# First squares of x earlier, weights of the value products 96 bytes further in longer rows, smaller first loads, and the last bank added in three parts

## The chip, the cores and the metric

The kernel runs on one core of one Trainium2 chip. The metric is the device time of one launch in microseconds (us), as the median of several runs. The engines are named as in the profile: PE (TensorE, with PEld for its weight loads), DVE (VectorE), ACT (ScalarE), POOL (GpSimd) and SP (SyncE, which here only starts DMAs).

## What is computed

One layer (DEPTH is 1) of a decoder trunk on 256 tokens of width 2048, in float32:

```python
h = rms_norm(x, g_mix)
qa, ka, va, qb, kb, vb, qc, kc, vc = split(h @ w_in)        # 2048 -> 6144
x = x + concat(diff_attention(qa, ka, va), moba_attention(qb, kb, vb), dilated_attention(qc, kc, vc)) @ w_out
x = x + memory_cross_attention(rms_norm(x, g_cross), rms_norm(mem, g_mem), w_cq, w_ckv, w_co)
x = x + conv_glu_ffn(rms_norm(x, g_ffn), w_up, conv_w, conv_b, w_down)   # d_ff 5632
out = rms_norm(x, g_final)
```

## The kernel before

**Tiling.** Every weight matrix is read once, in pieces of 1 MB (a tile `raw`, 128 partitions x 2048 floats, four buffers). A piece is worked off in two halves of 128 x 1024. Since PE multiplies at its fast rate only in the shortened type fp32r, each half is split into a high part (`hi`, made on ACT by `split_hi`) and the rest (`lo` = raw - hi, made on DVE by `split_lo`); each has five buffers of 128 x 1024. The activations are split in the same way (`hT`: 256 columns high, 256 columns low for each of 16 blocks of the contraction). A product then is high x high + low x high + high x low.

**Three forms of product.** `wstat_chunk` (q, k, w_out, w_up, ...) holds the weights still and streams `hT`: for each weight block one matmul over 512 columns (L295) and one over 256 (L302); where the 512 are not wanted together, L297, L298 and L302 do 256 each. `astat_chunk` (the values: three chunks of 512 columns and two of 256 from w_in, two of 256 from w_ckv) holds `hT` still and streams `hi`, `lo` and `hi` (L341 to L343). `down_mm` (w_down) holds the FFN's activations `ah`, `al` and streams `hi`, `lo`, `hi` (L851 to L853). In `astat_chunk` the streamed operand begins at the start of a `hi` or `lo` tile; in the layout of the program that start lies 64 bytes past a multiple of 128, for all ten tiles, and the held slices of `hT` lie 96 past one. In `wstat_chunk` it is the other way round (96 streamed, 64 held); in `down_mm` 64 streamed, 0 held.

**Order.** Every engine works its queue strictly in the order of the program, which the kernel writes by hand: a loop over the half pieces i runs `split_hi` for the half that is four ahead, the functions registered with `before(i)`, `split_lo`, the matmuls of half i, and those registered with `after(i)`. Chunk 0 is the first chunk of w_in (halves 0 to 7); its four results stand in four PSUM banks of the ring `acc` (five banks), and chunk 1 takes the fifth bank and then the four of chunk 0 again, each as soon as `merge` has read it: ACT copies one half of a bank to `mg` (L354), DVE adds the other (L355).

**The factor of x's norm** comes from `square_part` (ACT squares four blocks of x into `sq`, L223; for c = 1, 2, 3 DVE adds it to the first, L227) and `norm_factors` (DVE folds the sum twice, L236; PE sums over the partitions with two matmuls against `ones`, L241; DVE, POOL and PE make `rcol` and `rrow`). The parts stand behind halves 5, 6, 7 and 8, the fold before half 10.

**Start.** x comes in six loads by two or four blocks (`load_x`), mixed with the first pieces (`load_block` for two quarters of piece 0, `load_half` for halves, `load` for whole pieces from piece 3, which SP starts last of these). `put_x` makes the high and low part of two blocks of `hT`.

**End.** The last two pieces of w_down are worked off bank by bank (t is the half of the tokens, n the quarter of the columns): DVE adds the bank to x (L900), ACT squares the sum (`square_sum`, L265), DVE multiplies by the gain (`gained`, L873). For (t, n) = (1, 3) the last two pieces come in two halves of 256 columns: the first into the bank itself, the add then goes over all 512 columns; the second into a bank of its own, added over 256 (L902). Then POOL makes the factor (L915) and `finish` scales and stores: for t = 1 the quarters 0 and 1 on ACT (L862), 2 and 3 on DVE (L864), four stores of 256 KB (L869) on SP.

Of the kernel before, what the change touches and what calls it, by code (L numbers as in the profile page):

```python
# [11 lines left out]
F32 = mybir.dt.float32  # L12
# [50 lines left out]
def trunk(ctx, tc, x, mem, w_in, w_out, diff_lambda, rel_bias_table, w_cq, w_ckv, w_co, w_up, conv, w_down,  # L63
# [36 lines left out]
    class Piece:  # L100
        def __init__(self, srcs, mm, extra=None):
            self.srcs, self.mm, self.extra = srcs, mm, extra
            self.raw = None
            self.parts = [None, None]
# [33 lines left out]

    def split_hi(p, h):
        hi = wpool.tile([P, HALF], F32R, tag="hi", name="hi", bufs=NSPLIT)  # L140
        lo = wpool.tile([P, HALF], F32R, tag="lo", name="lo", bufs=NSPLIT)
# [137 lines left out]
    def wstat_chunk(w, col0, src, evac, korder=tuple(range(KD)), bank=acc_tile, wide=True):  # L279
# [5 lines left out]
        def mm(pi):  # L285
            def f(p, h):
# [18 lines left out]
                if cur[0] <= 2:  # L305
                    for f in (high, low):
                        for j in range(2):
                            for n in range(4):
                                f(n, j)
                    return  # L310
# [11 lines left out]
    def astat_chunk(w, col0, ncol, src, evac, korder):  # L322
# [25 lines left out]
        for pi in range(last + 1):  # L348
            pieces.append(Piece(sources(w, korder[pi * nk:(pi + 1) * nk], col0, ncol), mm(pi)))
# [496 lines left out]
    def down_mm(p, k, h, t, n, c0=0, c1=512, own=None):  # L846
# [6 lines left out]
        PE.matmul(o, al, wh, start=False, stop=(k == KF - 1))  # L853
# [4 lines left out]
    def finish(n, t, og, r):  # L858
        col = slice(n * 512, (n + 1) * 512)
        if t:  # L860
            if n < 2:
                ACT.activation(og[:, col], og[:, col], AF.Copy, scale=r)  # L862
            else:
                DVE.scalar_tensor_tensor(og[:, col], xtok(t, n), r, gfin["t"][:, col], op0=ALU.mult, op1=ALU.mult)  # L864
# [10 lines left out]
    def down(k):  # L875
        def f(p, h):
# [9 lines left out]
            elif k == KF - 1 and h == 1:  # L886
                done = None
                for t in range(NT):
# [5 lines left out]
                    for i, (n, c0, c1) in enumerate(parts_of):  # L894
                        own = any_tile()[:, :c1 - c0] if c0 else None
# [3 lines left out]
                        if own is None:  # L899
                            DVE.tensor_tensor(xtok(t, n), outs[t, n], xtok(t, n), op=ALU.add)  # L900
                        else:
                            DVE.tensor_tensor(xc, own, xc, op=ALU.add)  # L902
# [4 lines left out]
                        if not t or n < 2:  # L907
# [9 lines left out]
                for n in (2, 0, 3, 1):  # L917
                    finish(n, *done)
# [26 lines left out]
    load_x(0, 2)  # L945
    load_block(ACT, pieces[0], 0)
    load_block(SP, pieces[0], 1)
    ACT.copy(small(1, "first", 1), mhalf)
    load_x(2, 2)
    load_half(pieces[0], 1)  # L950
# [25 lines left out]
    put_x(0)  # L976
    p = pieces[0]
    p.parts[0] = hi, lo = [wpool.tile([P, HALF], F32R, tag=t, name=t, bufs=NSPLIT) for t in ("hi", "lo")]
# [102 lines left out]
```

## Time and profile before

| | |
|---|---|
| median of 3 runs | 1244.48 us (1242.91 to 1245.76) |
| the profiled execution | 1244.53 us, of it 1242.7 us span |
| PE busy | 1229.7 us, 99% of the span |
| DVE, ACT, POOL busy | 67%, 51%, 1% |
| mean granted clock of PE | 0.996 |
| HBM | 230 MB read, 2.1 MB written |

Times in rows count from the span's start; what lies outside the span is 1.8 us. A matmul's row shows its start and its modelled length; matmuls overlap, so their pace is read from one start to the next.

### The profile page before, as it was taken

The numbers are of one execution on the slowest core, as the hardware profiler recorded it, in microseconds if no ns is written. First come the engines' busy times: TensorE is split into PE (matmuls) and PEld (weight loads), VectorE is DVE, ScalarE is ACT, GpSimd is POOL, SyncE is SP. The second block draws the span as 40 slices with busy tenths as digits, with TensorE's granted clock in tenths as the row PEclk, the third lists the DMA queues.
The fourth block names the chain that finished last, engine by engine and source line by source line (L and its number), as shares of the span: only waits on it lengthen the run. The fifth ranks groups of instructions, "written<-read, shape, count | busy, mean of one in ns | idle before, by whom it ended". The sixth has DMA issues, their size and how long they took to land.

```text
span 1242.7 us, 17626 instructions
## 1 busy us (share of the span) xinstructions
PE 1229.7 (99%) x6934; PEld 1072.0 (86%) x6934; DVE 830.9 (67%) x1351; ACT 630.3 (51%) x981; POOL 14.2 (1%) x23
## 2 busy tenths in 40 slices
PE   8999999999999999999999999999999999999997
PEld 7888888988888899888888888888888888888885
DVE  7755667567568877776767768767677755554555
ACT  7445656556455656545444445444444544444444
POOL 0000000000000000000000000000000000000001
PEclk9999999999999999999999999999999999999998
DMA  9665554555566555565565565565656555555541
GB/s 345 209 195 190 175 178 163 184 168 173 177 216 218 170 169 166 202 206 173 169 203 183 190 198 178 182 203 190 197 176 203 185 188 204 180 192 203 180 160 68
DMA packets 104835, 233.26 MB, mean 188 GB/s; under 512 B 4208, under 2 KB 14768, under 8 KB 98992
## 3 DMA queue, kind: packets, MB, share of 16 engines
q1 hardware_dynamic: 104576, 231.85, 55.7%
q8 instruction: 54, 0.88, 0.3%
q10 hardware_dynamic: 144, 0.26, 0.1%
q14 instruction: 29, 0.24, 0.1%
q0 software_dynamic: 32, 0.02, 0.0%
HBM read 230.00 MB, written 2.12 MB: 187 GB/s over the span
## 4 chain that ended last, share of the span: by engine, by line
issue 58%; PE 37%; DVE 2%; DMA 1%; ACT 0%; POOL 0%; SPq 0%; POOLq 0%; DVEq 0%; ACTq 0%
PE acc L295 16%; PE acc L302 8%; PE acc L341 3%; PE acc L343 3%; PE acc L342 3%; DMA raw<-in_w_in 1%; PE at L401 1%; DVE lo L149 1%; PE at L420 0%; DMA xin<-in_x 0%; PE at L444 0%; PE acc L298 0%; PE acc L297 0%; DVE hT L197 0%; PE at L472 0%
## 5 line engine op out<-in xcount | busy, mean ns | idle before, releaser
L149 DVE TENSOR_TENSOR lo<-raw,hi 128x1024 fp32r<-128x1024 f32 x423 | 517.2, 1224 | 352.5 <-ACT hi L142 352.0
L142 ACT CAST hi<-raw 128x1024 fp32r<-128x1024 f32 x423 | 443.1, 1049 | 465.6 <-PE acc L295 273.3
L295 PE MATMUL acc<-hT,hi 128*128 128x512 f32 x1776 | 624.8, 394 | 2.5 <-DVE mg L355 1.9
L302 PE MATMUL acc<-hT,lo 128*128 128x256 f32 x1840 | 511.7, 280 | 0.0
L295 PEld LDWEIGHTS acc<-hT,hi 128*128 128x128 f32 x1776 | 334.0, 188 | 77.1 <-DVE mg L355 2.2
L302 PEld LDWEIGHTS acc<-hT,lo 128*128 128x128 f32 x1840 | 345.2, 188 | 0.3
L295 PE MATMUL at<-hT,hi 128*128 128x512 f32 x528 | 187.5, 392 | 0.0
L302 PE MATMUL at<-hT,lo 128*128 128x256 f32 x528 | 147.6, 280 | 0.0
L295 PEld LDWEIGHTS at<-hT,hi 128*128 128x128 f32 x528 | 99.2, 188 | 21.8
L302 PEld LDWEIGHTS at<-hT,lo 128*128 128x128 f32 x528 | 99.1, 188 | 0.0
L851 PE MATMUL acc<-hi,ah 128*128 128x512 f32 (+1 forms) x222 | 87.0, 392 | 0.0
L853 PE MATMUL acc<-hi,al 128*128 128x512 f32 (+1 forms) x222 | 86.6, 390 | 0.0
L852 PE MATMUL acc<-lo,ah 128*128 128x512 f32 (+1 forms) x222 | 85.7, 386 | 0.0
L341 PE MATMUL acc<-hi,hT 128*128 128x256 f32 (+1 forms) x224 | 75.0, 335 | 0.0
L343 PE MATMUL acc<-hi,hT 128*128 128x256 f32 (+1 forms) x224 | 73.9, 330 | 0.0
L342 PE MATMUL acc<-lo,hT 128*128 128x256 f32 (+1 forms) x224 | 73.8, 330 | 0.0
L788 ACT ACTIVATE y<-y 128x256 f32<-128x256 f32 x44 | 18.5, 419 | 66.4 <-DVE y L784 66.3
L851 PE MATMUL at<-hi,ah 128*128 128x512 f32 x132 | 52.0, 394 | 0.0
L853 PE MATMUL at<-hi,al 128*128 128x512 f32 x132 | 51.7, 392 | 0.0
L852 PE MATMUL at<-lo,ah 128*128 128x512 f32 x132 | 51.2, 388 | 0.0
L853 PEld LDWEIGHTS acc<-hi,al 128*128 128x128 f32 x222 | 41.7, 188 | 9.6
L852 PEld LDWEIGHTS acc<-lo,ah 128*128 128x128 f32 x222 | 41.7, 188 | 9.2
(159 smaller groups left out, 1005.0 us busy)
## 6 DMA issues: line engine op xcount, KB each, us to landing
raw<-in_w_up SPq DMA_DIRECT2D x88, 1024.0 KB, 5.1
raw<-in_w_in SPq DMA_DIRECT2D x45, 1024.0 KB, 5.2
raw<-in_w_down SPq DMA_DIRECT2D x44, 1024.0 KB, 4.9
raw<-in_w_out SPq DMA_DIRECT2D x12, 1024.0 KB, 5.2
raw<-in_w_ckv SPq DMA_DIRECT2D x8, 1024.0 KB, 5.3
raw<-in_w_out SPq DMA_DIRECT2D x8, 512.0 KB, 4.8
raw<-in_w_cq SPq DMA_DIRECT2D x4, 1024.0 KB, 5.3
raw<-in_w_co SPq DMA_DIRECT2D x4, 1024.0 KB, 5.3
```

The lines of the kernel that those rows point to most:

```text
L142: ACT.copy(hi, p.raw[:, h * HALF:(h + 1) * HALF])
L149: DVE.tensor_tensor(lo, p.raw[:, h * HALF:(h + 1) * HALF], hi.bitcast(F32), op=ALU.subtract)
L295: PE.matmul(accs[n], w, x, start=(i == 0), stop=False)
L302: PE.matmul(accs[n][:, :S], lo[:, j, n * P:(n + 1) * P], src()[:, korder[i], :S], start=False, stop=(i == len(korder) - 1))
L341: PE.matmul(o, xh, hi[:, j, :], start=(i == 0), stop=False)
L342: PE.matmul(o, xh, lo[:, j, :], start=False, stop=False)
L343: PE.matmul(o, xl, hi[:, j, :], start=False, stop=(i == len(korder) - 1))
L401: PE.matmul(out, a[u], b[w], start=first and i == 0, stop=last and i == 2)
L788: after(cur[0] + 1 + n, lambda: ACT.activation(gate[k], gate[k], AF.Silu))
L851: PE.matmul(o, ah, wh, start=(k == first), stop=False)
L852: PE.matmul(o, ah, wl, start=False, stop=False)
L853: PE.matmul(o, al, wh, start=False, stop=(k == KF - 1))
```

## The change

- Both kinds of split tile get rows of 1056 floats instead of 1024 (`part_tiles`), of which a piece uses 1024 from `shift` on; the pieces of `astat_chunk` get a shift of 24 floats, all others 0. The memory for it comes out of a scratch area that is made 8 KB smaller. In the new layout the ten tiles start 64 bytes past a multiple of 128 as before, the shifted operands 32 past one; the held slices of `hT` stay at 96 and of `ah`, `al` at 0. Each tile now starts 128 bytes further against `hT` than the tile before it; before, all had the same place within 4096 bytes.
- x's squares stand behind halves 1, 1, 3 and 4, so the adds before 2, 4 and 5, and the fold before 7, its matmuls behind 7.
- The first two blocks of x come in two loads and the second half of piece 0 in two; the preparation of piece 0 goes block by block, and half 0's matmuls too.
- Ahead of the last banks DVE adds bank (1, 3), which holds all but the last two pieces, to x; both of its halves then go to banks of their own and are added over 256 columns. For t = 1 only quarter 0 is multiplied by the gain ahead and finished on ACT; quarters 1 to 3 go to DVE. The quarters 2 and 0 are finished and stored in halves, six stores in all.

```diff
-        def __init__(self, srcs, mm, extra=None):
-            self.srcs, self.mm, self.extra = srcs, mm, extra
+        def __init__(self, srcs, mm, extra=None, shift=0):
+            self.srcs, self.mm, self.extra, self.shift = srcs, mm, extra, shift
...
+    def part_tiles(p):
+
+        return [wpool.tile([P, HALF + 32], F32R, tag=t, name=t, bufs=NSPLIT)[:, p.shift:p.shift + HALF] for t in ("hi", "lo")]
+
     def split_hi(p, h):
-        hi = wpool.tile([P, HALF], F32R, tag="hi", name="hi", bufs=NSPLIT)
-        lo = wpool.tile([P, HALF], F32R, tag="lo", name="lo", bufs=NSPLIT)
+        hi, lo = part_tiles(p)
         ACT.copy(hi, p.raw[:, h * HALF:(h + 1) * HALF])
         p.parts[h] = (hi, lo)
...
                 if cur[0] <= 2:
-                    for f in (high, low):
-                        for j in range(2):
-                            for n in range(4):
-                                f(n, j)
+                    for j, f in (((0, high), (0, low), (1, high), (1, low)) if cur[0] == 0 else
+                                 ((0, high), (1, high), (0, low), (1, low))):
+                        for n in range(4):
+                            f(n, j)
                     return
                 for n in range(4):
...
         for pi in range(last + 1):
-            pieces.append(Piece(sources(w, korder[pi * nk:(pi + 1) * nk], col0, ncol), mm(pi)))
+            pieces.append(Piece(sources(w, korder[pi * nk:(pi + 1) * nk], col0, ncol), mm(pi), shift=24))
...
-    def finish(n, t, og, r):
-        col = slice(n * 512, (n + 1) * 512)
-        if t:
-            if n < 2:
-                ACT.activation(og[:, col], og[:, col], AF.Copy, scale=r)
-            else:
-                DVE.scalar_tensor_tensor(og[:, col], xtok(t, n), r, gfin["t"][:, col], op0=ALU.mult, op1=ALU.mult)
+    def finish(n, t, og, r, c0=0, c1=512):
+        col = slice(n * 512 + c0, n * 512 + c1)
+        if t and n:
+            DVE.scalar_tensor_tensor(og[:, col], xtok(t, n)[:, c0:c1], r, gfin["t"][:, col], op0=ALU.mult, op1=ALU.mult)
         elif n < 2:
             ACT.activation(og[:, col], og[:, col], AF.Copy, scale=r)
         else:
...
             elif k == KF - 1 and h == 1:
                 done = None
+
+                DVE.tensor_tensor(xtok(1, 3), outs[1, 3], xtok(1, 3), op=ALU.add)
...
                     parts_of = ((0, 0, 512), (1, 0, 512), (2, 0, 512)) + (((3, 0, 256), (3, 256, 512)) if t else ((3, 0, 512),))
                     for i, (n, c0, c1) in enumerate(parts_of):
-                        own = any_tile()[:, :c1 - c0] if c0 else None
+                        own = any_tile()[:, :c1 - c0] if (t, n) == (1, 3) else None
                         for kk in range(KF - TAIL, KF):
                             down_mm(fin[kk], kk, n // 2, t, n % 2, c0, c1, own)
                         xc = xtok(t, n)[:, c0:c1]
                         if own is None:
-                            DVE.tensor_tensor(xtok(t, n), outs[t, n], xtok(t, n), op=ALU.add)
-                        else:
-                            DVE.tensor_tensor(xc, own, xc, op=ALU.add)
+                            own = outs[t, n][:, c0:c1]
+                        DVE.tensor_tensor(xc, own, xc, op=ALU.add)
                         square_sum(xc, ss[:, i:i + 1], c1 - c0)
                         if done:
                             for m in ((2, 0), (3, 1), (), (), ())[i]:
                                 finish(m, *done)
-                        if not t or n < 2:
+                        if not t or n < 1:
                             gained(og, t, n)
...
-                for n in (2, 0, 3, 1):
-                    finish(n, *done)
+                for n, c0, c1 in ((2, 0, 256), (0, 0, 256), (2, 256, 512), (0, 256, 512), (3, 0, 512), (1, 0, 512)):
+                    finish(n, *done, c0, c1)
...
-    load_x(0, 2)
+    load_x(0, 1)
     load_block(ACT, pieces[0], 0)
+    load_x(1, 1)
     load_block(SP, pieces[0], 1)
     ACT.copy(small(1, "first", 1), mhalf)
     load_x(2, 2)
-    load_half(pieces[0], 1)
+    load_block(SP, pieces[0], 2)
+    load_block(SP, pieces[0], 3)
     load_x(4, 2)
     load_half(pieces[1], 0)
...
-    put_x(0)
+    def put_high(k):
+        high(xblock(k), MIX, lambda: hT["h"], k)
+
+    def put_low(k):
+        low(xblock(k), MIX, lambda: hT["h"], k)
+
...
     p = pieces[0]
-    p.parts[0] = hi, lo = [wpool.tile([P, HALF], F32R, tag=t, name=t, bufs=NSPLIT) for t in ("hi", "lo")]
-    for j in range(2):
-        c = slice(j * 512, (j + 1) * 512)
-        ACT.copy(hi[:, c], p.raw[:, c])
-        DVE.tensor_tensor(lo[:, c], p.raw[:, c], hi[:, c].bitcast(F32), op=ALU.subtract)
-    put_x(2)
-    split(1)
+    for h in range(2):
+        p.parts[h] = hi, lo = part_tiles(p)
+        if h:
+            put_high(2)
+            put_high(3)
+        for j in range(2):
+            k = 2 * h + j
+            c = slice(j * 512, (j + 1) * 512)
+            r = p.raw[:, h * HALF + j * 512:h * HALF + (j + 1) * 512]
+            if h == 0:
+                put_high(k)
+            n = 2 if k == 0 else 1
+            for i in range(n):
+                w = 512 // n
+                ACT.copy(hi[:, j * 512 + i * w:j * 512 + (i + 1) * w], r[:, i * w:(i + 1) * w])
+            put_low(k)
+            DVE.tensor_tensor(lo[:, c], r, hi[:, c].bitcast(F32), op=ALU.subtract)
     load(pieces[3])
     nload = 4
 
     for i in range(3):
         for j in range(2):
             after(i, lambda h=2 * i + j: (put_x(2 * h + 4), split(h + 2)))
+
     for c in range(4):
-        square_part(c + 5, "x", c, lambda c=c: xpart(c))
-    norm_factors(10, "x")
+        square_part((1, 1, 3, 4)[c], "x", c, lambda c=c: xpart(c))
+    norm_factors(7, "x")
...
     arrays = {f"in_{name}": np.ascontiguousarray(a) for name, a in arrays.items()}
-    nc = bacc.Bacc("TRN2", target_bir_lowering=False, num_devices=1)
+    nc = bacc.Bacc("TRN2", target_bir_lowering=False, num_devices=1, dynamic_dma_scratch_size=8192)
...
```

On DVE before, around the end of chunk 0 (`lo` is a split half, `hT` two low parts of x's blocks, `sq` an add of squares, `mg` the merges that free chunk 0's banks); the first row is the first half of piece 3:

```order
L149 TENSOR_TENSOR lo<-raw,hi 128x1024
L197 SCALAR_TENSOR_TENSOR hT<-xin,hT 128x256 x2
L149 TENSOR_TENSOR lo<-raw,hi 128x1024 x4
L227 TENSOR_TENSOR sq<-sq 128x1024
L149 TENSOR_TENSOR lo<-raw,hi 128x1024
L355 TENSOR_TENSOR mg<-acc,mg 128x256 x4
L227 TENSOR_TENSOR sq<-sq 128x1024
L149 TENSOR_TENSOR lo<-raw,hi 128x1024
```

And now, from the same half on:

```order
L152 TENSOR_TENSOR lo<-raw,hi 128x1024
L200 SCALAR_TENSOR_TENSOR hT<-xin,hT 128x256 x2
L152 TENSOR_TENSOR lo<-raw,hi 128x1024
L230 TENSOR_TENSOR sq<-sq 128x1024
L152 TENSOR_TENSOR lo<-raw,hi 128x1024
L230 TENSOR_TENSOR sq<-sq 128x1024
L152 TENSOR_TENSOR lo<-raw,hi 128x1024 x2
L239 TENSOR_TENSOR sq<-sq 128x512
L239 TENSOR_TENSOR sq<-sq 128x256
L152 TENSOR_TENSOR lo<-raw,hi 128x1024
L358 TENSOR_TENSOR mg<-acc,mg 128x256 x4
```

The first of the three adds went ahead of these rows; between piece 3's first half and the merges stand the same six split halves, two adds instead of one, and the two folds.

On ACT now, from the second half of piece 2 on (`hi` is a split half, `sq` a square of four blocks of x, `hT` two high parts of x's blocks, `mg` the merges' copies):

```order
L145 CAST hi<-raw 128x1024
L226 ACTIVATE sq<-xin 128x1024 x2
L197 ACTIVATE hT<-xin 128x256 x2
L145 CAST hi<-raw 128x1024
L197 ACTIVATE hT<-xin 128x256 x2
L145 CAST hi<-raw 128x1024
L226 ACTIVATE sq<-xin 128x1024
L145 CAST hi<-raw 128x1024
L226 ACTIVATE sq<-xin 128x1024
L145 CAST hi<-raw 128x1024 x3
L357 COPY mg<-acc 128x256 x4
```

Two squares moved ahead of piece 3's first half (the second cast here), and two into the row of casts behind it, where before the first two squares stood further back.

On PE now, at the end of chunk 0 (the last two rows of it, then the norm's two matmuls, then chunk 1):

```order
L298 MATMUL acc<-hT,hi 128x512
L305 MATMUL acc<-hT,lo 128x256
L244 MATMUL at<-ones,sq 128x1 x2
L298 MATMUL acc<-hT,hi 128x512
L305 MATMUL acc<-hT,lo 128x256
```

The norm's matmuls, which need the folds, came three halves of chunk 1 forward, to its very front.

## Rows read from the trace of the kernel before

**Rows 1.** Timeline of PE around 30 us: start us, us, engine, line, tiles [idle before]
```profile
31.36 0.71 PE L295 MATMUL acc<-hT,hi 128*128 128x512 f32 x1 [1.88 <-DVE mg L355]
```

**Rows 2.** Busy time by stretch: busy us (count) of each engine, PEclk, DMA, GB/s
```profile
4.00:20.80 16.80, 16.16 (x97) 14.12 (x96) 12.94 (x21) 12.05 (x21) 0.00 (x0) 1.00 1.04 390
...
31.50:34.90 3.40, 3.40 (x11) 2.92 (x12) 3.40 (x6) 1.87 (x2) 0.00 (x0) 0.50 1.01 336
```

**Rows 3.** Timeline of DVE, 21 to 39 us
```profile
21.92 1.23 DVE L149 TENSOR_TENSOR lo<-raw,hi 128x1024 fp32r<-128x1024 f32 x1 [2.36 <-ACT hi L142]
...
23.85 4.85 DVE L149 TENSOR_TENSOR lo<-raw,hi 128x1024 fp32r<-128x1024 f32 x4
28.62 1.22 DVE L227 TENSOR_TENSOR sq<-sq 128x1024 f32<-128x1024 f32 x1
...
30.89 1.41 DVE L355 TENSOR_TENSOR mg<-acc,mg 128x256 f32<-128x256 f32 x4
...
37.42 1.15 DVE L236 TENSOR_TENSOR sq<-sq 128x512 f32<-128x512 f32 x2
```

**Rows 4.** Timeline of ACT, the first half of piece 3
```profile
20.83 1.05 ACT L142 CAST hi<-raw 128x1024 fp32r<-128x1024 f32 x1 [2.69 <-DMA raw<-in_w_in]
```

**Rows 5.** Timeline of PE, first product and start of half 6
```profile
6.21 0.96 PE L295 MATMUL acc<-hT,hi 128*128 128x512 f32 x3 [0.64 <-DVE hT L197]
...
23.08 0.39 PE L295 MATMUL acc<-hT,hi 128*128 128x512 f32 x1
```

**Rows 6.** Timeline of PE, values, 512 columns: first and last of 31
```profile
84.14 0.40 PE L341 MATMUL acc<-hi,hT 128*128 128x512 f32 x1
...
91.14 0.40 PE L341 MATMUL acc<-hi,hT 128*128 128x512 f32 x1
```

**Rows 7.** Timeline of PE, values, 256 columns: first and last of 61
```profile
103.83 0.28 PE L341 MATMUL acc<-hi,hT 128*128 128x256 f32 x1
...
111.03 0.28 PE L341 MATMUL acc<-hi,hT 128*128 128x256 f32 x1
```

**Rows 8.** Timeline of PE, w_down: first and last of 43
```profile
1059.75 0.39 PE L851 MATMUL at<-hi,ah 128*128 128x512 f32 x1
...
1069.36 0.39 PE L851 MATMUL acc<-hi,ah 128*128 128x512 f32 x1
```

**Rows 9.** Timeline of PE, w_up: first and last of 41 (20 pairs between)
```profile
639.89 0.39 PE L295 MATMUL acc<-hT,hi 128*128 128x512 f32 x1
...
646.82 0.39 PE L295 MATMUL acc<-hT,hi 128*128 128x512 f32 x1
```

**Rows 10.** Timeline of PE, scores of the memory's attention
```profile
451.02 0.88 PE L401 MATMUL at<-qk 128*128 128x256 f32 x6
451.73 0.88 PE L401 MATMUL acc<-qk 128*128 128x256 f32 x6
```

**Rows 11.** Groups of PE's instructions by line and shape: count, busy us, mean ns
```profile
L295 PE MATMUL acc<-hT,hi 128*128 128x512 f32 x1776 | 624.8, 394 | 2.5 <-DVE mg L355 1.9 <-DVE hT L197 0.6
L295 PE MATMUL at<-hT,hi 128*128 128x512 f32 x528 | 187.5, 392 | 0.0
L341 PE MATMUL acc<-hi,hT 128*128 128x512 f32 x96 | 38.6, 402 | 0.0
L341 PE MATMUL acc<-hi,hT 128*128 128x256 f32 x128 | 36.4, 284 | 0.0
```

**Rows 12.** The end: timelines of DVE, ACT and SP, and the stores' group
```profile
1224.06 0.69 DVE L900 TENSOR_TENSOR xin<-acc,xin 128x512 f32<-128x512 f32 x1 [1.81 <-PE acc L853]
...
1234.77 0.42 ACT L265 ACTIVATE junk<-xin 128x256 bf16<-128x256 f32 x1
...
1236.16 1.41 DVE L864 SCALAR_TENSOR_TENSOR raw<-xin,rfin,gfin 128x512 f32<-128x512 f32 x2 [0.69 <-POOL rfin L915]
1236.94 1.80 SPq L869 DMA_DIRECT2D out<-raw  x4
DMA to landing us min/median/max: 2.4/2.9/3.3
```

More of the change, by code (lines that the diff above doesn't have):

```diff
@@ L852, in down_mm @@
         PE.matmul(o, ah, wl, start=False, stop=False)
-        PE.matmul(o, al, wh, start=False, stop=(k == KF - 1))
+        PE.matmul(o, al, wh, start=False, stop=k == KF - 1 or (own is None and (t, 2 * h + n, k) == (1, 3, KF - TAIL - 1)))
     ss3 = small(10, "ss3", 1)
     fin = {}
-    def finish(n, t, og, r):
-        col = slice(n * 512, (n + 1) * 512)
-        if t:
-            if n < 2:
-                ACT.activation(og[:, col], og[:, col], AF.Copy, scale=r)
-            else:
-                DVE.scalar_tensor_tensor(og[:, col], xtok(t, n), r, gfin["t"][:, col], op0=ALU.mult, op1=ALU.mult)
+    def finish(n, t, og, r, c0=0, c1=512):
+        col = slice(n * 512 + c0, n * 512 + c1)
+        if t and n:
+            DVE.scalar_tensor_tensor(og[:, col], xtok(t, n)[:, c0:c1], r, gfin["t"][:, col], op0=ALU.mult, op1=ALU.mult)
         elif n < 2:
```

## The prediction

> **What bounds the kernel now.** PE is busy for 99% of the span, so a change pays only where it takes time out of PE's queue, at the two ends, or in PE's pace. I read first who PE waits for, then the timelines at those places, then the pace of each form of product.
>
> PE waits twice after its warm-up [rows 11]. Before its first product it waits 0.64 us [rows 5]. At the front of chunk 1 it waits 1.88 us for the merge that frees a bank of chunk 0, and starts again at 31.36 [rows 1]. Just then its granted clock falls: from 31.5 to 34.9 it is 0.50, the 1.2 GHz level [rows 2]. 3.5 us at half rate lose 1.75 us, so this place costs 3.6 us in all. The merge is late because DVE is late: the first half of piece 3 lands so that ACT can begin only at 20.83, after 2.69 idle [rows 4], DVE gets it at 21.92, and from there works without a gap until the merges at 30.89 [rows 3].
>
> **The squares: a longer wait, +1.7 us.** DVE idles 2.36 us before 21.92 [rows 3]. The first of the three adds now falls into this gap: the two squares run on ACT in its 2.69 idle us [rows 4], and the add is then done by about 20.5. That part is good, but more comes forward than fits into the gap. In front of the merges DVE still has, from 21.92 on, the same six split halves and two low parts of x, and now two adds where it had one, and both folds, which stood behind. An add takes (30.89 - 28.62) / 2 = 1.13 us with the half behind it taken as equal, the folds 1.15 [rows 3]. Piece 3 cannot land sooner (below), so nothing of this moves ahead of 21.92. ACT has no more to do in this stretch than before (two squares, as then), and its last square waits for the second add at about 26.2, which delays it by 0.6, but the casts stay ahead of DVE. The merges begin at 30.89 + 1.13 + 1.15 = 33.2, and PE's second column block at 33.2 + (31.36 - 30.89) = 33.6 instead of 31.36: 2.3 us later. On top, the norm's two matmuls now stand at the front of chunk 1 in PE's queue and wait for the folds, until about 32; behind them is queued the first column block (0.7 us), for which a bank is free. It still ends before 33.6 at the full clock, so this order costs nothing more.
>
> What the clock adds or gives back depends on where its low stretch lies. If it again lasts from 31.5 to 34.9, PE stands idle in a part of it: before, PE had by 34.9 done 0.7 + 3.5 / 2 = 2.5 us of full-rate work of chunk 1, now (34.9 - 32.2) / 2 = 1.4, so the loss is 1.1 us. If it lasts as long from PE's restart as it did before, the loss is the full 2.3. If it comes twice, 1.75 more: 4.0. No row ties the stretch to one of these; I take the middle of the first two, **+1.7** (1.1 to 4.0).
>
> **The values: a faster pace, -2.3 us.** The trace gives the pace of each form from two rows far apart. Values of 512 columns: 7.00 us for 30 matmuls, 233.3 ns [rows 6]; of 256 columns: 7.20 for 60, 120.0 ns [rows 7]. w_down, 512 columns: 9.61 for 42, 228.8 ns [rows 8]. A pair of 512 and 256 in w_up: 6.93 / 20 = 346.5 ns [rows 9], which leaves 117.7 for the 256. So the values are slower by 4.5 and 2.3 ns per matmul, with the same shapes, types and clock. What differs is where the operands begin within 128 bytes, as (streamed, held): w_up (96, 64) and w_down (64, 0) are fast, the values (64, 96) slow, and so are the scores of the memory's attention, (96, 96): six of 256 columns in 451.73 - 451.02 = 0.71 us, 118 to 119 ns each [rows 10]. The change makes the values (32, 96). Counted as held minus streamed, the fast forms have 96 and 64, the slow ones 32 and 0, and the change gives 64, that of w_down. By this reading all value products reach the fast pace: each of three lines has 96 matmuls of 512 columns and 128 of 256 [rows 11], so 288 x 4.5 + 384 x 2.3 = 1.30 + 0.88 = 2.2 us; with the disturbed stretches, whose mean is higher, **-2.3** (0 to -3). All of it is PE's own time, on the path. The other reading is that the held operand alone decides (0 and 64 fast, 96 slow); then nothing is gained. That is the second rival.
>
> The Trainium skill speaks for nothing here: "TensorE: Matmul & The Clock Gate", section Step-by-step: what each phase is for, says that PE reads its streamed and its held operand through two independent SBUF ports, so that a weight load takes no bandwidth from the running matmul. The trace doesn't bear out that the place is indifferent, since forms of one shape differ by 2%; by the page alone the sum would be 2.3 us higher, as in the second rival.
>
> **Longer rows: 0.** With 4224 bytes per tile, every tile lies 128 bytes further against `hT`. All other forms keep their places within 128 bytes, but not within 256 or 512. The trace has only one place within 512 for each form, so no row shows whether it matters. I take 0, since the four readings above go with the place within 128, and make the rest a rival.
>
> **The first loads: 0.** The PE warm-up ends at about 5.6, so at most 0.64 us can be gained [rows 5], and probably most of it is: the first block of x is waited for alone. But half 6 begins at 23.08 [rows 5] right where DVE's part of piece 3 is done (21.92 + 1.23) [rows 3]. DMA is full all the way to there (390 GB/s, share 1.04) [rows 2], and the change loads the same bytes ahead of piece 3 (two DMAs more, which SP starts long before their turn). PE thus arrives up to 0.6 us sooner at half 6 and waits there for the same data: 0 (0 to -0.6).
>
> **The end: -0.3 us.** The early add of bank (1, 3) runs in DVE's 1.81 us idle ahead of 1224.06 [rows 12] and is hidden. DVE loses a multiplication and half an add, but not DVE sets the factor: ACT squares and scales in one row without a gap up to the last square at 1234.77 [rows 12], and its queue is unchanged, so the factor is ready at 1236.1 as before. Behind it the first store needs half of a 512-column step (1.41 / 2 = 0.70) [rows 12] instead of a whole one and starts about 0.3 sooner. Before, four stores start at a pitch of about 0.47 from 1236.94 [rows 12]; now six follow, the last 0.8 - 0.3 + 5 x 0.47 = 2.8 us behind the factor instead of 2.2. A store that finds the queues free lands after 2.4 us, the last one, behind others, after 3.3 [rows 12]. The last now finds less ahead of it: 2.8 + 2.4 = 5.2 against 2.2 + 3.3 = 5.5, **-0.3** (-0.4 to +0.6, the latter if it takes 3.3 again).
>
> **Sum.** 1244.5 (the profiled execution, 0.05 from the median) + 1.7 - 2.3 - 0.3 = **1243.6 us**; its own range, with the bounds above, is 1242 to 1245.5. A run of this kernel can be told from no change beyond about 0.2%, 2.5 us here, so faster means under 1242.0 and slower over 1247.0: I forecast no change that can be measured.
>
> **Rivals.**
> (1) *The wait goes away* (1238.3 us, chance 0.2). Purpose of moving the squares: if the merges start by about 29.3, PE loses neither the 1.88 nor the 1.75 us. 1244.5 - 3.6 - 2.3 - 0.3. For it: two squares and an add do leave the crowded stretch for an idle one. Against: DVE's queue in front of the merges grows by 2.3 us of work. It needs piece 3 to land some 4 us sooner than DMA's rate gives; a part of it, one us for each us that piece 3 lands sooner.
> (2) *The shift gives nothing* (1245.9 us, chance 0.27): the held operand decides, and the values keep 233 and 120 ns. 1244.5 + 1.7 - 0.3. For it: the held place 96 is in both slow forms and in no fast one. This is also where the page above ends.
> (3) *The longer rows slow the other products* (1251.8 us, chance 0.07). Place: all pairs L295 and L302, 1776 + 528 of them [rows 11]. If the pace hangs on more than the place within 128 bytes, some of the five buffers fall on slow places; at the values' excess of 6.8 ns for a pair, all would cost 15.7 us, half of them 8. From a fifth of the pairs on the kernel is slower by over 0.2%. Against: nothing in the trace moves with it, and w_down at another place within 512 is as fast as w_up.
>
> **How the numbers follow.** The forecast has 0.46. Faster: rival 1 but for a small part (0.17) and the forecast's lower end with a gain in the first loads (0.10): 0.27. Slower: rival 3 (0.06), rival 2 with the low clock coming twice (0.08), the forecast's upper end (0.02): 0.16. Same: 0.57. The range takes in the forecast, rival 2 and the upper part of rival 1: 1240.0 to 1247.0.
>
> **What would show it.** PE's idle time at the front of chunk 1: about 3 us ahead of the norm's matmuls, released by the folds, and a short one released by the merge at 33 to 34; DVE without a gap from 21.9 to there. An idle time under 1 us there would prove the walk through DVE's queue wrong. The pace of L344 to L346: 229 and 118 ns, or 233 and 120 if rival 2 holds. Pairs at 346.5 ns and w_down at 229 ns show the longer rows harmless. PE's first product before 6.0 and a wait at half 6 show the first loads swallowed. Last store landing 5.2 us behind the factor.

## The result and the profile after

The changed kernel takes 1253.95 us (median; 1253.63 to 1254.17) against 1243.7 (1242.88 to 1245.76) of the kernel before in the same session: ratio 1.008, 95% interval 1.0062 to 1.0097. It is 10 us slower; the prediction said 1243.6 and held its range to 1240 to 1247. Of the sixteen runs of the kernel before that stand beside the fifth and sixth experiments, twelve take 1242.8 to 1243.2 us at a mean granted clock of 0.997 to 0.998 and four 1244.7 to 1245.2 at 0.996 to 0.997, and its profiled execution (1244.53 us at 0.996, with the low clock of [rows 2]) is like these four.

The first lines of the page of after; PE is still busy all the time, with as many instructions, only longer:

```profile
span 1252.4 us, 17640 instructions
...
PE 1239.0 (99%) x6934; PEld 1073.8 (86%) x6934; DVE 832.2 (66%) x1354; ACT 629.9 (50%) x983; POOL 15.1 (1%) x23
```

Where the time went is read from three starts on PE: the first value product, the first product of w_down, the last matmul. Timeline of PE, before (start us, us, engine, line, tiles):

```profile
78.55 0.39 PE L341 MATMUL acc<-hi,hT 128*128 128x512 f32 x1
...
991.75 0.40 PE L851 MATMUL acc<-hi,ah 128*128 128x512 f32 x1
...
1233.40 0.28 PE L853 MATMUL acc<-hi,al 128*128 128x256 f32 x1
```

The same three in after (its lines stand 3 further down):

```profile
81.50 0.40 PE L344 MATMUL acc<-hi,hT 128*128 128x512 f32 x1
...
999.56 0.40 PE L854 MATMUL acc<-hi,ah 128*128 128x512 f32 x1
...
1243.19 0.28 PE L856 MATMUL acc<-hi,al 128*128 128x256 f32 x1
```

Up to the first value product after loses 2.95 us. From there to the first product of w_down it takes 918.06 instead of 913.20 (+4.86), in w_down 243.63 instead of 241.65 (+1.98), behind the last matmul 1252.4 - 1243.19 = 9.21 instead of 1242.7 - 1233.40 = 9.30 (-0.09). The sum, 9.7, is the difference of the spans.

What changed in these two parts is the pace. Timeline of PE in after: w_up, two starts 40 pairs apart; values of 512 columns, 30 matmuls apart; of 256, 60 apart; w_down, 90 apart:

```profile
659.72 0.39 PE L298 MATMUL acc<-hT,hi 128*128 128x512 f32 x1
...
673.72 0.39 PE L298 MATMUL at<-hT,hi 128*128 128x512 f32 x1
...
84.28 0.40 PE L344 MATMUL acc<-hi,hT 128*128 128x512 f32 x1
...
91.21 0.39 PE L344 MATMUL acc<-hi,hT 128*128 128x512 f32 x1
...
103.70 0.28 PE L344 MATMUL acc<-hi,hT 128*128 128x256 f32 x1
...
110.77 0.28 PE L344 MATMUL acc<-hi,hT 128*128 128x256 f32 x1
...
1099.96 0.40 PE L854 MATMUL acc<-hi,ah 128*128 128x512 f32 x1
...
1120.73 0.39 PE L854 MATMUL acc<-hi,ah 128*128 128x512 f32 x1
```

| form | before | after |
|---|---|---|
| pair of 512 and 256, w_up | 346.5 ns [rows 9] | 14.00 us / 40 = 350.0 |
| values, 512 columns | 233.3 [rows 6] | 6.93 / 30 = 231.0 |
| values, 256 columns | 120.0 [rows 7] | 7.07 / 60 = 117.8 |
| w_down | 228.8 [rows 8] | 20.77 / 90 = 230.8 |

The values gained 288 x 2.3 + 384 x 2.2 = 1.5 us. The 1408 pairs of w_up lost 1408 x 3.5 = 4.9, w_down lost 1056 x 2.0 = 2.1.

The front of chunk 1, timeline of PE (idle time and its releaser in brackets), then of DVE, in after:

```profile
31.84 1.02 PE L244 MATMUL at<-ones,sq 128*128 128x1 f32 x4 [2.94 <-DVE sq L239]
```

```profile
30.64 1.14 DVE L239 TENSOR_TENSOR sq<-sq 128x512 f32<-128x512 f32 x2
...
32.83 1.41 DVE L358 TENSOR_TENSOR mg<-acc,mg 128x256 f32<-128x256 f32 x4
```

PE waits 2.94 us for the folds (L239) where it waited 1.88 for a merge [rows 1], and the merges (L358) start at 32.83 instead of 30.89 [rows 3]. Busy time by stretch in after (PE, PEld, DVE, ACT, POOL, then PEclk, DMA share, GB/s): the clock is low for two such stretches, before for one [rows 2]:

```profile
31.50:34.90 3.40, 3.06 (x11) 2.77 (x12) 3.40 (x8) 0.56 (x1) 0.50 (x1) 0.50 0.99 322
34.90:38.30 3.40, 3.40 (x12) 2.92 (x11) 0.54 (x1) 0.30 (x1) 1.11 (x1) 0.50 0.75 283
```

### The profile page after: what moved, and what is told of

Same layout as the page of the kernel before. It is cut to its first block, busy times and chain, and to the rows that moved or that the text cites. A ratio compares the mean times of both kernels' runs of the same rounds, so it can differ in the third digit from the quotient of the medians.

```text
span 1252.4 us, 17640 instructions
## 1 busy us (share of the span) xinstructions
PE 1239.0 (99%) x6934; PEld 1073.8 (86%) x6934; DVE 832.2 (66%) x1354; ACT 629.9 (50%) x983; POOL 15.1 (1%) x23
## 4 chain that ended last, share of the span: by engine, by line
issue 58%; PE 38%; DVE 2%; DMA 0%; POOL 0%; ACT 0%; SPq 0%; POOLq 0%; DVEq 0%; ACTq 0%
PE acc L298 17%; PE acc L305 9%; PE acc L344 3%; PE acc L346 3%; PE acc L345 3%; PE at L404 1%; DVE lo L152 1%; PE at L423 0%; PE at L447 0%; DMA xin<-in_x 0%; PE acc L301 0%; PE acc L300 0%; PE at L475 0%; DVE hT L200 0%; POOL raw L868 0%
```

## The experiments

### 1 to 3: which part costs what

**The rows alone**, on the kernel before (so in all three places that make the tiles). The scratch area is 8 KB smaller in all three of these kernels, so it parts none of them from another:

```diff
-        hi = wpool.tile([P, HALF], F32R, tag="hi", name="hi", bufs=NSPLIT)
+        hi = wpool.tile([P, HALF + 32], F32R, tag="hi", name="hi", bufs=NSPLIT)[:, :HALF]
```

> The kernel before, with one edit: the ten split tiles get rows of 1056 floats, all pieces begin at the row's start (no shift), and the scratch area is 8 KB smaller to make room. Theory A, the rows are the cause: each tile now starts 128 bytes further within 512 against the other operand, and the trace of the changed kernel has its w_up pairs at about 349.5 ns instead of 346.5 and its w_down products at 230.8 instead of 228.8. Then this edit alone gives (2304 pairs x 3 ns = 6.9) + (1056 x 2 ns = 2.1) = 9 us, so about 1252 to 1253, with the wait at the front of chunk 1 as before (1.9 us). Theory B, something else in the changed kernel slows PE for good (the low clock near 35 us, another order): then pairs stay at 346.5 and the time at 1243.7 within 1 us.

Measured: 1251.42 us, ratio 1.0068 (1.0053 to 1.0083), that is +8.5 us (6.6 to 10.3). Timeline of PE in w_up, 40 pairs apart:

```profile
659.78 0.40 PE L295 MATMUL acc<-hT,hi 128*128 128x512 f32 x1
...
673.78 0.40 PE L295 MATMUL acc<-hT,hi 128*128 128x512 f32 x1
```

14.00 / 40 = 350.0 ns, as in after, and w_down takes 243.63 us from its first product to the last matmul, also as in after. The longer rows, without any shift, are most of the loss: theory A.

**All but the rows**, on the changed kernel:

```diff
-        return [wpool.tile([P, HALF + 32], F32R, tag=t, name=t, bufs=NSPLIT)[:, p.shift:p.shift + HALF] for t in ("hi", "lo")]
+        return [wpool.tile([P, HALF], F32R, tag=t, name=t, bufs=NSPLIT)[:, p.shift:p.shift + HALF] for t in ("hi", "lo")]
...
-            pieces.append(Piece(sources(w, korder[pi * nk:(pi + 1) * nk], col0, ncol), mm(pi), shift=24))
+            pieces.append(Piece(sources(w, korder[pi * nk:(pi + 1) * nk], col0, ncol), mm(pi)))
```

> The changed kernel with the split tiles put back to rows of 1024 floats and no shift; squares, first loads, order of half 0 and the last banks stay as changed. Theory A (rows are the cause of most): pairs back at 346.5, w_down at 228.8, the values at 233.3 and 120.0; what is left is the front, which in the changed kernel reaches the first value product at 81.50 us instead of 78.55, of it 0.6 by slower pairs: +2.4 us, and the end, 0.2 longer. Expected 1246 (1245 to 1247). Theory B (another part slows PE): 1250 or more.

Measured: 1246.39 us (before, in the same session, 1243.1), ratio 1.0032 (1.0018 to 1.0047), +4.0 us (2.2 to 5.8): theory A. The same three starts on PE as above:

```profile
79.88 0.39 PE L344 MATMUL acc<-hi,hT 128*128 128x512 f32 x1
...
993.04 0.40 PE L854 MATMUL acc<-hi,ah 128*128 128x512 f32 x1
...
1234.68 0.28 PE L856 MATMUL acc<-hi,al 128*128 128x256 f32 x1
```

913.16 us to w_down and 241.64 in it, as before (913.20 and 241.65): with the old rows the paces are the old ones, and all that is left of the loss stands ahead of the first value product. The two parts make 8.5 + 4.0 = 12.5 us, more than the 10 measured; the intervals cover the difference, and the shift, which gains, is in neither of the two kernels.

**Rows that keep one place within 512 bytes**, with the shift, on the kernel before:

```diff
+        hi = wpool.tile([P, HALF + 128], F32R, tag="hi", name="hi", bufs=NSPLIT)[:, p.shift:p.shift + HALF]
...
-            pieces.append(Piece(sources(w, korder[pi * nk:(pi + 1) * nk], col0, ncol), mm(pi)))
+            pieces.append(Piece(sources(w, korder[pi * nk:(pi + 1) * nk], col0, ncol), mm(pi), shift=24))
```

> The kernel before, with rows of 1152 floats (4608 bytes, a multiple of 512) and the value pieces begun 24 floats (96 bytes) further; scratch 8 KB smaller. All tiles keep one place within 512 bytes, 64 below a multiple; the shifted operands lie 32 past one, against held slices at 96. Theory A1 (the place within 512 decides, and 'held minus streamed' of 64 is the fast one): pairs 346.5, w_down 228.8, values fall to 229 and 118: 1243.7 - 2.2 = 1241.5. Theory A2 (the held slices alone decide for the values): nothing changes, 1243.7. Theory A3 (places above 512 bytes matter too, since 4608 moves them as well): pairs go to 349, 1250 or more.

Measured: 1240.74 us, ratio 0.9982 (0.9973 to 0.9992): 2.2 us faster (1.0 to 3.4), as A1 said, but not in the way it said. Timeline of PE: w_up 40 pairs apart, values of 512 columns 30 matmuls, of 256 columns 60 matmuls apart:

```profile
659.69 0.39 PE L295 MATMUL at<-hT,hi 128*128 128x512 f32 x1
...
673.55 0.39 PE L295 MATMUL at<-hT,hi 128*128 128x512 f32 x1
...
84.19 0.39 PE L341 MATMUL acc<-hi,hT 128*128 128x512 f32 x1
...
91.19 0.39 PE L341 MATMUL acc<-hi,hT 128*128 128x512 f32 x1
...
101.99 0.28 PE L341 MATMUL acc<-hi,hT 128*128 128x256 f32 x1
...
108.79 0.28 PE L341 MATMUL acc<-hi,hT 128*128 128x256 f32 x1
```

Pairs 13.86 / 40 = 346.5, unharmed, also with the smaller scratch area. Values of 512 columns 7.00 / 30 = 233.3: no gain at all. Values of 256 columns 6.80 / 60 = 113.3 instead of 120.0, 384 x 6.7 = 2.6 us: more than the "fast" pace that the prediction knew. Neither of its two readings has room for this.

### 4: the place, measured by itself

256 groups, each a line of its own, like this one (`held` and `strm` both start at a multiple of 512 bytes; "held minus streamed" is the distance in bytes from where the streamed operand begins to where the held one does):

```python
for i in range(16): PE.matmul(bank, held[:, 24 + i % 2 * P:24 + i % 2 * P + P], strm[:, 0:512], start=i == 0, stop=i == 15)  # held 96, streamed 0
```

> No layer at all: everything is left out but 256 groups of 16 matmuls (512 columns, fp32r, a weight load before each, two held blocks in turn), one group for each pair of places in steps of 32 bytes within 512: held operand 0 to 480, streamed operand 0 to 480; the output is filler. Theory A (place of one operand against the other decides): the pace of a group is a function of held minus streamed, within 128 or within 512 bytes, with about 229 at differences of 64 and 96 and 233 at 0 and 32 if 128 is the measure. Theory A2: the pace is a function of the held place alone (0 and 64 fast, 96 slow). Rival: the pace is the same in all groups, and the differences in the kernels come from other engines' traffic in the memory.

Timeline of PE; L83 to L92 hold the weights at 0, 32, ... 288 and stream from 0 (four of the ten left out). Start to start, by 16, is the pace:

```profile
15.72 3.80 PE L83 MATMUL bank<-strm,held 128*128 128x512 f32 x16
19.35 3.89 PE L84 MATMUL bank<-strm,held 128*128 128x512 f32 x16
...
38.00 3.84 PE L89 MATMUL bank<-strm,held 128*128 128x512 f32 x16
41.68 3.89 PE L90 MATMUL bank<-strm,held 128*128 128x512 f32 x16
45.40 3.80 PE L91 MATMUL bank<-strm,held 128*128 128x512 f32 x16
49.04 3.89 PE L92 MATMUL bank<-strm,held 128*128 128x512 f32 x16
```

L83 (0) has 3.63 / 16 = 226.9 ns, L89 (192) 3.68 / 16 = 230.0, L90 (224) 3.72 / 16 = 232.5, and L91, at 256, is back at 3.64 / 16 = 227.5. All 256 groups follow it: the pace depends on held minus streamed modulo 256 bytes, and on nothing else of the two places (groups of one difference stand within 0.4 ns of their median, but for 12 that are up to 2 ns off, most of them just behind a jump in the list).

| held minus streamed, mod 256 | 0 | 32 | 64 | 96 | 128 | 160 | 192 | 224 |
|---|---|---|---|---|---|---|---|---|
| 512 columns, ns | 227.2 | 232.8 | 233.4 | 233.8 | 232.3 | 233.3 | 229.9 | 232.8 |

So "modulo 128" was wrong, and so was "the held place alone", and the rival that other engines' traffic does it: no other engine works here. The table gives the values before (96 - 448, that is 160 modulo 256: 233.3) and in the third experiment (64: 233.4), which the prediction had called a move to the fast place, and nearly w_down (192: 229.9, in the kernel 228.8). In after the ten tiles fall on two differences each, 128 apart, since a row is 4224 bytes, so its paces need not stand in the table. Triples (streamed high, low, high, as in the values and w_down) with the high part at 64 and the low part at 192 take 230.8 ns by themselves in the seventh experiment, the other way round 230.3; after's values of 512 columns take 231.0 and its w_down 230.8. This does not cover its values of 256 columns: they take 117.8, not a mean of the two places' 113.8 and 117.7, and why, no run shows.

### 5 and 6: the squares

**The move alone**, on the kernel before:

```diff
-        square_part(c + 5, "x", c, lambda c=c: xpart(c))
-    norm_factors(10, "x")
+        square_part((1, 1, 3, 4)[c], "x", c, lambda c=c: xpart(c))
+    norm_factors(7, "x")
```

> The kernel before with the move of x's squares alone (behind halves 1, 1, 3, 4, fold before half 7); tiles, loads and end as before. Theory A (the move is the cost that the second experiment left, +3.3): PE waits about 3 us for the folds at the front of chunk 1 instead of 1.9 for the merge, its clock falls at about 31.5 and stays low for 3.4 or 6.8 us, first value product about 80 us; 1246 to 1247. Theory B (the finer loads or the split last bank cost it): 1243.7 within 1.

Measured: ratio 1.0027 (1.0016 to 1.0038), +3.4 us (2.0 to 4.7): theory A. **Only the first add moved:**

```diff
+        square_part((1, 1, 7, 8)[c], "x", c, lambda c=c: xpart(c))
```

> The kernel before with only the first add of squares moved (squares behind halves 1, 1, 7, 8 instead of 5, 6, 7, 8; fold before half 10 as before). It takes one add (1.13 us) out of DVE's row ahead of the merges and puts nothing in: merges from 29.8, PE's wait at the front of chunk 1 about 0.75 instead of 1.88. Theory A (the wait is set by DVE's row, so the idea of the move is right and only its amount wrong): 1242.0 to 1242.6, and 1.75 less if the low clock does not come. Theory B (the wait is set by what the trace puts down to it only by accident): 1243.1.

Measured: ratio 0.9989 (0.9979 to 0.9998), 1.4 us faster (0.2 to 2.6): theory A. PE's start of chunk 1, the clock and the first value product of the move alone (two low stretches), then PE's start and the clock of the first add alone:

```profile
32.23 1.01 PE L241 MATMUL at<-ones,sq 128*128 128x1 f32 x4 [3.16 <-DVE sq L236]
...
31.50:34.90 3.40, 2.67 (x9) 2.44 (x10) 3.37 (x9) 0.94 (x1) 0.11 (x1) 0.57 0.95 312
34.90:38.30 3.40, 3.40 (x12) 2.86 (x11) 0.93 (x1) 0.00 (x0) 1.50 (x1) 0.50 0.80 298
...
81.55 0.39 PE L341 MATMUL acc<-hi,hT 128*128 128x512 f32 x1
```

```profile
30.15 0.50 PE L295 MATMUL acc<-hT,hi 128*128 128x512 f32 x1 [0.16 <-DVE mg L355]
...
31.50:34.90 3.40, 3.40 (x21) 2.99 (x20) 3.40 (x4) 2.10 (x3) 0.00 (x0) 1.00 1.06 403
```

The wait was DVE's row, as read: with one add and the two folds more in front of the merges than before it is 3.16 us, and the clock stays low for two stretches; with one add less than before it is 0.16 us (0.75 was expected), and the clock stays up.

### 7, 9 and 10: pairs have a rhythm, not only a place

The seventh measured the kernel's own forms by themselves. A place of a pair is given as (high, low): held minus streamed of the high part, which streams 512 columns, and of the low part, which streams 256; the kernel before has (96, 96).

> No layer: everything is left out but groups of matmuls at chosen places, the output is filler. Four forms: 512 and 256 columns with all operands at one difference of held minus streamed, in steps of 8 bytes within 256; pairs of 512 and 256 with the two held parts at 8 x 8 differences; triples as in w_down and the values, streamed hi, lo, hi against held h, h, l, at 8 x 8 x 4 differences. Theory (from the fourth experiment: the pace depends on held minus streamed modulo 256 bytes): 512 columns 227.2 at 0 and 233.4 at 64 as there, nothing new in steps below 32; pairs at (96, 96) 346.5 as in the kernel before; triples at 160 233.3 and at 192 229; 256 columns 120.0 at 160 and 113.3 at 64, as the values before and in the third experiment. If one of these four does not come out, the place within 256 is not the whole cause in the kernel.

256 columns: 119.9 ns at 160 and 113.8 at 64, as the values before and in the third experiment. Triples 233.6 at 160 and 229.9 at 192. Pairs at (96, 96), the kernel's: 346.7. All four came out. Of the 64 places of pairs, 63 lie between 346.4 and 353.8; one, (64, 0), is far below, L167. The ninth was to see whether that lasts:

> No layer: everything is left out but groups of 8 pairs (512 and 256 columns, as in w_up) at 32 x 32 places, held high and held low part in steps of 8 bytes within 256 against a fixed streamed operand; the output is filler. Theory: the points of the seventh experiment come again, (96, 96) at 346.7 and (64, 0) at 340.1, and these are within 1 ns of the same here though other groups run ahead of them. Rival: 340.1 there was left by the group ahead of it, and (64, 0) now gives 346 or more. Between the steps of 32 nothing under 340 is expected.

It does not last. Timeline of PE, place (64, 0), in the seventh (starts 11 pairs apart) and the ninth experiment (7 pairs apart):

```profile
263.26 0.39 PE L167 MATMUL bank<-sa,ha 128*128 128x512 f32 x1
...
267.00 0.39 PE L167 MATMUL bank<-sa,ha 128*128 128x512 f32 x1
```

```profile
731.91 0.39 PE L341 MATMUL bank<-sa,ha 128*128 128x512 f32 x1
...
734.36 0.39 PE L341 MATMUL bank<-sa,ha 128*128 128x512 f32 x1
```

3.74 / 11 = 340.0 and 2.45 / 7 = 350.0 ns, the same instructions at the same places: the rival's case. Other places now have 340 over the whole group: (192, 0), which had 350.0 in the seventh, and between the steps of 32 (64, 16), (64, 40), (64, 144) and (64, 216). None is under 340, as expected. The tenth put short disturbances ahead of each place:

> No layer: everything is left out but rows of 10 pairs (512 and 256 columns) at 24 places, each place 24 times, behind one of 24 short disturbances (one to three transposes, one or two products of 256 or 512 columns at other places); the output is filler. In the candidate the pairs of w_up hold 340 ns for 300 us without a break, while the pairs of w_in among the heads' small products stand mostly at 348 to 357. Theory (a place has more than one stable rhythm, and what runs ahead of a row of pairs sets which): (64, 0) shows about 340 behind some disturbances and about 350 behind others, to the end of the row; some other place, (64, 16), (64, 40), (64, 144), (64, 216), (192, 0) by the ninth experiment, falls to 340 behind most or all. Rival (the slow pairs in w_in come from DVE, ACT or DMA traffic of that stage): (64, 0) shows 340 behind all of them, here where no other engine works.

Timeline of PE: (64, 0) behind one transpose (L89) and behind one product of 256 columns (L95); each time the second and the tenth start, 8 pairs apart:

```profile
15.53 0.39 PE L89 MATMUL bank<-sa,ha 128*128 128x512 f32 x1
...
18.25 0.39 PE L89 MATMUL bank<-sa,ha 128*128 128x512 f32 x1
...
26.55 0.39 PE L95 MATMUL bank<-sa,ha 128*128 128x512 f32 x1
...
29.34 0.39 PE L95 MATMUL bank<-sa,ha 128*128 128x512 f32 x1
```

2.72 / 8 = 340 and 2.79 / 8 = 349. No other engine works here, so the rival falls. Counted over the 24 disturbances, by the last four pairs of each row, for five of the 24 places:

| place (high, low) | at 340 ns | else |
|---|---|---|
| (64, 0) | 6 of 24 | 350 to 353 |
| (64, 216) | 23 | 354 |
| (192, 0) | 22 | 350 |
| (216, 144) | 24 | |
| (96, 96), the kernel's | 0 | 346 to 347, all 24 |

### 8, 11 and 12: the places put to use

Rows of 1088 floats (4352 bytes, 17 x 256) keep all ten tiles at one place modulo 256; each kind of piece gets its own start, chosen so that held minus streamed is what the runs before found best:

```diff
-        def __init__(self, srcs, mm, extra=None):
+        def __init__(self, srcs, mm, extra=None, shift=(56, 40)):
...
+        return [wpool.tile([P, HALF + 64], F32R, tag=t, name=t, bufs=NSPLIT)[:, s:s + HALF]
+                for t, s in zip(("hi", "lo"), p.shift)]
...
-            pieces.append(Piece(sources(w, korder[pi * nk:(pi + 1) * nk], col0, ncol), mm(pi)))
+            pieces.append(Piece(sources(w, korder[pi * nk:(pi + 1) * nk], col0, ncol), mm(pi), shift=(40, 40) if ncol == 512 else (24, 24)))
...
-        pieces.append(Piece([src], down(k), (lambda k=k: a_high(k), lambda k=k: a_low(k))))
+        pieces.append(Piece([src], down(k), (lambda k=k: a_high(k), lambda k=k: a_low(k)), shift=(48, 48)))
```

> The kernel before with places chosen by the seventh experiment, rows of 1088 floats (4352 bytes, a multiple of 256, so that all buffers keep one place), and the first add of squares moved as in the sixth. Held minus streamed modulo 256: pairs 64 for the high part and 0 for the low part (hi starts 224 bytes, lo 160 bytes into its row), values of 512 columns 0, of 256 columns 64, w_down 0. Theory (place within 256 decides, in the kernel as by itself): pairs 340 instead of 346.5, 2304 of them, -14.8 us; values 288 x 6 = -1.7 and 384 x 6.7 = -2.6; w_down 1056 x 1.8 = -1.9; first add -1.1: 1243 - 22 = 1221. Rival (other engines' traffic takes the place's gain, or DVE and ACT slow down on shifted rows and PE must wait for them): w_up's halves, 8 pairs each, would be limited by DVE or the loads; the pace of the pairs stays above 344, 1232 or more.

Measured: 1229.16 us, ratio 0.9889 (0.9872 to 0.9905). Better than any kernel so far, but 8 us short of the theory. Timeline of PE in the stage of the heads: two starts 22 pairs apart, then, behind some small products, two 6 apart:

```profile
149.77 0.40 PE L298 MATMUL acc<-hT,hi 128*128 128x512 f32 x1
...
157.47 0.40 PE L298 MATMUL acc<-hT,hi 128*128 128x512 f32 x1
...
161.53 0.39 PE L298 MATMUL acc<-hT,hi 128*128 128x512 f32 x1
...
163.57 0.39 PE L298 MATMUL acc<-hT,hi 128*128 128x512 f32 x1
```

7.70 / 22 = 350 and 2.04 / 6 = 340 ns: at (64, 0) the pairs are in one rhythm ahead of a head's small products and in the other behind them. The values of 256 columns fell short too: at 64, where the third experiment has 113.3, their first stage stands at 117.7 here and in the eleventh; why, no run shows. The pairs led to the tenth experiment, and with (216, 144) from it (`shift=(30, 12)` for the pairs) to the eleventh:

> The candidate of the eighth experiment with the pairs at another place: held minus streamed 216 for the high part and 144 for the low part (hi starts 120 bytes, lo 48 bytes into its row); all else as there. In the tenth experiment this place fell to 340 ns behind all 24 disturbances, (64, 0) behind 6. Theory (the rhythm of the pairs is set by their place and by what runs ahead): the 592 pairs of the candidate that stood at 348 to 357 come to about 341, -5 us: 1224. Rival (their pace there comes from other engines): 1229 as the candidate.

Measured: **1222.28 us**, ratio 0.9829 (0.9815 to 0.9842): 21 us faster than the kernel before, some 31 faster than after, the theory's case. Counted over the whole trace, pairs at 348 ns or more fall from 550 in the eighth kernel to 77. The same stage, two starts 18 pairs apart (340 ns):

```profile
166.27 0.39 PE L298 MATMUL acc<-hT,hi 128*128 128x512 f32 x1
...
172.39 0.39 PE L298 MATMUL acc<-hT,hi 128*128 128x512 f32 x1
```

The twelfth adds the change's first loads and its split last bank to that:

> The kernel of the run beside it plus the two parts of the change that are left: first loads and half 0 block by block, and the last bank in three parts with six stores. It separates these from all else. Expected from the prediction's own terms, which no run has yet parted from the squares: first loads 0 (PE starts 0.7 us sooner and is late again at half 6), end -0.3 (in the changed kernel and the second experiment the span ends 9.2 us behind PE's last matmul, before 9.3): 0 to -0.4 against the run beside it. If it is more than 1 us better, the first loads do reach the end once the front of chunk 1 is mended; if it is worse by 1 us or more, one of the two parts has a cost of its own.

Measured: 1222.27 us, ratio 0.9831 (0.9818 to 0.9844): the same as the eleventh. What these two parts are worth lies within the noise, 1.6 us either way in each ratio.

## Why the prediction was wrong

**Longer rows: 0.** This is the step that failed, and rival 3 (given 0.07) is what happened; its price, 1243.6 + 8, is 1251.6 and not 1251.8. The term was put at nothing because "the four readings above go with the place within 128". They did so by accident: of eight differences modulo 256, four forms gave four points, and each form has its own table. The pairs at (96, 96) had been taken as fast and divided into 228.8 and 117.7 by borrowing w_down's pace; alone, 512 columns at 96 take 233.8, the slowest of all, and pairs can run at 340. Paces of different forms can't be laid on one scale: only one form at two places shows what a place does, and the trace of before held no such case. The honest value of this step was its bound, up to +15.7, with far more than 0.07. Its price came out near: the edit alone is +8.5, the rival had 8 for half of the pairs; in truth it is 3.5 ns in the mean of w_up's pairs, and 2.0 on each matmul of w_down, which the rival didn't count. So the price was near by luck; the cause, a place that counts beyond 128 bytes, was the rival's. The range was too narrow as well: the bounds stated at the terms add up to 1241.6 to 1249.1, not to 1242 to 1245.5 (neither holds the measured time).

**The values: -2.3.** The kernel got 1.5: 2.3 ns for each matmul of 512 columns, where 4.5 were forecast, and 2.2 of 256, where 2.3 were. With one place for all, the 512 columns gain nothing and the 256 columns 2.6: that the sum comes near the term is luck, the reason for it was wrong. Rival 2 was wrong too, since the 256 columns moved with the held place unchanged.

**The squares: +1.7.** The walk through DVE's row held: a wait of about 3 us released by the folds was forecast and is 2.94, merges at 33.2 and they start at 32.83. The second, short wait, for the merge, did not come: with the clock low, PE is still at the norm's matmuls and the first column block when the merge is done. What failed is the size: the term is the middle of two cases with one low stretch of the clock, and the third, "if it comes twice 1.75 more: 4.0", happened in after and in the fifth experiment (+3.4). The second experiment, with a wait of 3.15 us, has one, a little later (0.59 and 0.90 in the two stretches); its row for the stretch that is all low in the other two:

```profile
34.90:38.30 3.40, 3.40 (x20) 2.96 (x20) 0.92 (x2) 1.05 (x1) 1.25 (x1) 0.90 0.77 287
```

Its first value product comes at 79.88, that of the fifth at 81.55, that of before, with one low stretch too, at 78.55. So in these executions the move costs 1.3 us with one stretch and 3.0 with two, where the prediction had 1.1 to 2.3 and 4.0; how many come, no row could tell.

**The first loads: 0** held: the first product starts earlier (5.48 instead of 6.21 [rows 5]), chunk 1 does not, and the twelfth run shows nothing gained. The wait at half 6 that was to swallow the lead is not in after, whose lead is used up before: its half 1 takes 2.38 us for eight products of 512 columns where half 2 takes 2.02, and its pairs are slower. It is in the twelfth experiment (0.38 us) and in the second, in half 6's first pair:

```profile
23.23 0.38 PE L305 MATMUL acc<-hT,lo 128*128 128x256 f32 x1 [0.27 <-DVE lo L152]
```

The pair behind it starts at 23.45, in before at 23.42: there the mechanism was as forecast.

**The end: -0.3** was -0.1 in the profile, too little for any run to show in its time.

The Trainium skill ("TensorE: Matmul & The Clock Gate", Step-by-step: what each phase is for) states that PE reads its two operands through two independent ports. Taken as a rule that the place of an operand makes no difference, this would have the fourth experiment flat. It measured 227.2 to 233.8 ns there, by place alone with no other engine at work, so here the measurement decides against such a rule. What inside PE or the memory makes the difference, no run shows.

## What to carry to other kernels

An edit that moves buffers in memory is an edit to every instruction that reads them: before taking it as free, ask for each form whether the trace shows that form at the new place, and if it doesn't, let the bound carry weight. Keep the pitch of a ring of buffers that PE reads a multiple of 256 bytes (4224 bytes cost 8.5 us here, 4608 nothing), and choose where the operands begin by a small run of the same sequence of instructions, with the interruptions that it has in the kernel. When work is moved forward, count what now stands in front of the first thing that the bound engine waits for; here one add moved gained and three lost.

## What was not expected of the hardware

- PE's pace hangs on held minus streamed start modulo 256 bytes: 227.2 to 233.8 ns for 512 columns in steps of 32, 113.6 to 121.5 for 256 in steps of 8 (seventh experiment). Why the steps are as they are, no run shows.
- A row of pairs at one place can run at 340 or at 350 ns to the end of the row, by what ran ahead (tenth experiment). In the candidate of the eighth run the pairs of w_up stood at 340 to the end of the stage, those among the heads changed from one to the other.
- The low clock: behind waits of about 3 us it was seen in all three kernels that have them, for 3.4 us in the second experiment and 6.8 in after and the fifth; behind 1.9 us it was seen in before [rows 2] and not in the third experiment, which waits 1.85 us at the same place, nor behind 1.21 us in the first. What decides there stays open.
